# Small query tiles first in the attention, a denser rest of the query projection, and 16 high-part copies moved from ScalarE to VectorE

## The chip, the cores and the metric

The kernel runs on one core of one Trainium2 chip. The metric is the device time of one execution in microseconds (us). A core has engines that run side by side, each working through its own instructions in order: TensorE (PE, matrix products and transposes; PEld is its weight load), VectorE (DVE), ScalarE (ACT), GpSimd (POOL) and SyncE (SP, here only a queue of transfers). TensorE writes to PSUM, and VectorE and ScalarE read its results there.

## What is computed

The reference is a two-layer decoder trunk over 512 positions of width 1024, all in float32. Layer 0 mixes with a gated recurrence and a retention, layer 1 with a sparse attention of three branches; each layer ends in a SwiGLU feed-forward part. The change lies in the attention of layer 1. For each query position it computes three attentions and adds them with gates:

```
s = einsum('bqgrd,bngd->bgrqn', qb, kc)            # compressed keys, 31 of them
o_cmp = softmax(s, masked) @ vc
s = einsum('bqgrd,bgqkld->bgrqkl', qb, kg)         # selected blocks: all 8 blocks are selected (top_k = 8)
o_slc = softmax(s, causal) @ vg
s = einsum('bqgrd,bkgd->bgrqk', qb, kw)            # window of 512 positions
o_win = softmax(s, causal) @ vw
o = gb[..., 0:1] * o_cmp + gb[..., 1:2] * o_slc + gb[..., 2:3] * o_win
out = o @ w_out
```

There are 16 heads in 4 groups that share keys and values. With 512 positions the selected and the window branch both come to plain causal attention, each with its own keys and values. They are called branch 0 and branch 1 below.

## The kernel before

Float32 products are made of three products of a reduced type: each operand is split into a high part (a copy that rounds) and a low part (operand minus high part), and high times high, high times low and low times high are added in PSUM (`mm3`, lines 201 to 203). ScalarE makes most high parts and VectorE most low parts.

The 512 queries are four tiles of 128. A query tile `i` sees `i + 1` key blocks of 128, so tile 0 is small and tile 3 large. `attention` cuts the work into units: one group of 4 heads of one tile, with one branch (tiles 2 and 3) or with both (tiles 0 and 1). That makes 4 units for each of tiles 0 and 1, 8 for each of tiles 2 and 3, 24 in all. The order is `tiles = halves[0] + halves[1]`, before (2, 3, 1, 0).

The main loop counts `n` over units. In each step it goes through slots `sl`, at least four. A slot does, in the order of the code: a score of one head of unit `n` (`head_s`, lines 1160 to 1162: two products against the keys' high and low part and one that adds the causal mask, into a tile `ps_s`); for one block of unit `n - 3` (`LAG = 3`) four transposes of probabilities into `ps_tr` (`block_t`, L1185); the score's maximum on VectorE (`head_m`, `nm`, L1166); the high part of the transposed block on ScalarE (`block_hi`, `pth`, L1189); the exponentials on ScalarE, with their sums (`head_e`, `prob`, L1170); the block's low part on VectorE (`block_lo`, `ptl`, L1192); the scaling of one head of unit `n - 1` on GpSimd (`scale`, L1180); and two products of an earlier block into the output (`block_v`, `ps_o`, L1200 and L1201). After a group's last block `finish` adds the two halves of the output (`up` on ScalarE, `o` on VectorE, L1217, two instructions of 64 rows) and splits it (`oh` on ScalarE, `ol` on GpSimd).

Two side streams run in the slots. `side` holds generators that advance one or two steps a slot: the compressed branch of a tile (`compressed`, `pcmp`, lines 1099 to 1131), `finish`, and `late(t)`, which transposes and splits the queries of a later tile (stacking, `qs`, L1017, L1022, L1023). `fill` is the second half of the query projection (heads 8 to 15), tile by tile, 24 products a tile into `ps_t`; one step is 6 products or the taking over of a finished tile. Before, one step of `fill` is done in a slot. The queries of `halves[0]` are stacked as soon as they are projected, three steps late (`flush`); those of `halves[1]` are kept in `qlate` until `late(t)`.

The code's order is not the last word: a scheduler orders each engine's instructions, with the hints of `prio`. The probabilities' tiles share the pool `wr` (4 buffers) with the raw weights, so the first weights of the output projection (`w1o`, then `ps_p`, lines 201 to 203) are loaded when the first of the last four units has been transposed, and then split (`whi` L136 on ScalarE, `wlo` L137 on VectorE).

Of the kernel before, what the change touches and what calls it, by code (L numbers as in the profile page):

```python
# [63 lines left out]
class Trunk:  # L64
# [773 lines left out]
    def layer1(self, hg):  # L838
        nc, a, tc = self.nc, self.a, self.tc
        V, A, Q, T = nc.vector, nc.scalar, nc.gpsimd, nc.tensor  # L840
# [164 lines left out]
            VV.append(vv)  # L1005


        halves = ((2, 3), (1, 0))
        QS = {t: self.b8([P, H, P], F32R, name="qs") for t in halves[0]}
        qlate = self.b8([P, 2, H, DH], name="qlate")  # L1010

# [14 lines left out]
        def by_tile(w, ts):  # L1026
            for t in ts:
                ps = self.psA("ps_t")
                cc = slice(t * P, (t + 1) * P)
                for k0 in range(0, KD, 2):  # L1030
                    self.mm3(ps, [(HH(k)[:, cc], HL(k)[:, cc]) + w[k // 4].at(k % 4 * S, (k % 4 + 1) * S) for k in (k0, k0 + 1)], k0 == 0, k0 == KD - 2)
                    yield t, None
                flush(0)
                yield t, ps

        def queries(c, tiles):
            for t, ps in tiles:
                if ps is None:
                    if c == 0:
                        flush()  # L1040
                    yield
                    continue
                late = t in halves[1]
                qt = qlate[:, halves[1].index(t), 8 * c:8 * c + 8, :] if late else self.g2([P, 8, DH], name="qt")
                A.activation(qt, ps.rearrange("p (h d) -> p h d", h=8), AF.Copy, scale=r8[:, t:t + 1])
                self.rope(qt, 8, self.pcos[:, t, :], self.psin[:, t, :])
                if not late:
                    deferred.append((now, lambda t=t, qt=qt: stack(t, qt.rearrange("p h d -> p (h d)"), c)))
                yield
            if c:  # L1050
                flush(0)
# [3 lines left out]
        fill = queries(1, by_tile([self.unit(), self.unit()], halves[0] + halves[1]))  # L1055
# [22 lines left out]
    def attention(self, QS, stack, stacked, qlate, halves, KH, KL, VV, kc2, vc, gate, OH, OL, fill):  # L1078
# [3 lines left out]
        V, A, Q, T = nc.vector, nc.scalar, nc.gpsimd, nc.tensor  # L1082
# [52 lines left out]
        def late(t):  # L1135
            QS[t] = self.b8([P, H, P], F32R, name="qs")
            for c in range(2):
                stack(t, qlate[:, halves[1].index(t), 8 * c:8 * c + 8, :].rearrange("p h d -> p (h d)"), c)
                yield
# [11 lines left out]
        def head_s(u, r):  # L1151
            if r == 0:
                u.p = self.probs().rearrange("p (r b x) -> p r b x", r=R, b=u.n)
                u.rs = self.sm.tile([P, R, u.n], F32, tag="rs", name="rs")
                u.kh, u.kl = (x[u.g // 2][:, u.bs[0]:u.bs[-1] + 1, u.g % 2, 0:u.nk] for x in (KH, KL))
            h = R * u.g + r
            ps = self.psA("ps_s")
            u.ps = ps[:, 0:u.n * u.nk].rearrange("p (b x) -> p b x", b=u.n)
            q = QS[u.i][:, h, :]
            T.matmul(u.ps, q, u.kh, start=True, stop=False)  # L1160
            T.matmul(u.ps, q, u.kl, start=False, stop=False)
            T.matmul(u.ps[:, :, u.i * P:u.nk], self.identr, self.triNeg.unsqueeze(1).broadcast_to([P, u.n, P]), start=False, stop=True)

        def head_m(u, r):
            u.nm = self.sm.tile([P, 2], F32, tag="nm", name="nm")
            V.tensor_reduce(u.nm[:, 0:u.n], u.ps, axis=AX.X, op=ALU.max, negate=True)  # L1166

        def head_e(u, r):
            for b in range(u.n):
                A.activation(u.p[:, r, b, 0:u.nk], u.ps[:, b, :], AF.Exp, bias=u.nm[:, b:b + 1], accum_out=u.rs[:, r, b:b + 1])  # L1170
# [11 lines left out]
        def block_t(u, b, j):  # L1182
            u.pt = self.psC("ps_tr")
            for r in range(R):
                T.transpose(u.pt[:, r * P:(r + 1) * P], u.p[:, r, b, j * P:(j + 1) * P], self.ident)  # L1185
            u.th, u.tl = (self.g2([P, S], F32R, name="pt" + n) for n in "hl")

        def block_hi(u, b, j):
            A.copy(u.th, u.pt)  # L1189

        def block_lo(u, b, j):
            V.tensor_tensor(u.tl, u.pt, u.th.bitcast(F32), op=ALU.subtract)  # L1192
            u.last = u.th, u.tl
# [36 lines left out]
        def advance():  # L1230
            if side and next(side[0], 0) == 0:
                side.pop(0)
                advance()

        LAG = 3
        prio = self.tc.high_priority
        pend = []
        for n in range(len(units) + LAG):
            us = units[n] if n < len(units) else None
            un = units[n - 1] if 0 <= n - 1 < len(units) else None  # L1240
            uv = units[n - LAG] if n >= LAG else None
            if us is not None and us.g == us.bs[0] == 0:
                at = tiles.index(us.i)
                if at + 1 < NT:
                    t = tiles[at + 1]
                    side += ([late(t)] if t in halves[1] else []) + [compressed(t)]
            nb = len(uv.blocks) if uv else 0
            for sl in range(max(R, nb)):
                hd = us.heads[sl] if us and sl < R else None
                bl = uv.blocks[sl] if sl < nb else None  # L1250
                while us and (us.i, us.g // 2) not in stacked:
                    if next(fill, 0) == 0:
                        advance()
                if hd:
                    head_s(*hd)
                if bl:
                    block_t(*bl)
                if hd:
                    with prio(offset=12):
                        head_m(*hd)  # L1260
                if bl:
                    block_hi(*bl)
                if hd:
                    with prio(offset=-6):
                        head_e(*hd)
                if bl:
                    with prio(offset=-12):
                        block_lo(*bl)
                if un and sl < R:
                    if sl == 0:  # L1270
                        with prio(offset=-6):
                            norm(un)
                    scale(un, sl)
                if len(pend) >= 2:
                    args = pend.pop(0)
                    block_v(*args)
                    u, b, j = args[:3]
                    if u.bs[b] == 1 and j == u.i:
                        side.insert(0, finish(u.i, u.g))
                if bl:  # L1280
                    pend.append(bl + uv.last)
                for _ in range(2 if len(side) > 2 else 1):
                    advance()
                next(fill, 0)
        while pend:
            block_v(*pend.pop(0))
        while side:
# [136 lines left out]
```

## Time and profile before

| | us |
|---|---|
| median of 3 runs (lowest to highest) | 1250.39 (1248.1 to 1251.37) |
| the profiled execution | 1249.32 |
| its span in the trace | 1247.3 |
| TensorE products busy in the span | 1224.3 (98%) |
| TensorE weight loads busy | 1034.7 (83%) |
| VectorE busy | 800.6 (64%) |
| ScalarE busy | 679.8 (54%) |
| GpSimd busy | 231.6 (19%) |

The span is the trace's; the profiled execution's time lies 2.0 us above it. Times in the trace count from the span's start. Shares over the whole span are means over stages of different kinds, so what the attention does is read from its own stretch, 674 to 853 us. In the trace, the durations of instructions that follow each other on an engine overlap; how far is read from their starts.

### The profile page before, as it was taken

To read this page: it belongs to the slowest core of one execution; us is meant where nothing else is said; L and a number is where in the kernel's file an instruction comes from. 1 tells how busy PE (TensorE), PEld (TensorE's weight loads), DVE (VectorE), ACT (ScalarE), POOL (GpSimd) and SP (SyncE) were. 2 spreads that over 40 slices of the span, in tenths; PEclk is the share of its full clock that TensorE was granted. 3 is DMA by queue.
4 is the path that set the end of the run, shared out by engine and by line. 5 is a ranking of instruction groups with operands and counts; after the bars stand their busy time and mean duration, and the time that the engine had idled before them with its cause. 6 is when DMAs were issued, how large, how long until landed. Compare 5 with 4: busy or idle time off the path is not lost.

```text
span 1247.3 us, 16450 instructions
## 1 busy us (share of the span) xinstructions
PE 1224.3 (98%) x6077; PEld 1034.7 (83%) x6077; DVE 800.6 (64%) x1247; ACT 679.8 (54%) x1385; POOL 231.6 (19%) x303
## 2 busy tenths in 40 slices
PE   9999999999999999999999999999999999999996
PEld 7688888888888889987888878877888888889986
DVE  6886629666356636674364889986776546654765
ACT  6541337664256426655454688995666336633651
POOL 0000420220012002100000568680111011101200
PEclk9999999999999999999999999999999999999998
DMA  8121043784478438852100000133488358825832
GB/s 341 68 101 68 35 169 102 172 185 150 102 182 184 134 69 177 223 198 75 66 35 1 1 1 1 35 122 150 113 191 198 110 125 184 195 89 103 180 84 68
DMA packets 35567, 149.23 MB, mean 120 GB/s; under 512 B 3968, under 2 KB 6288, under 8 KB 26656
## 3 DMA queue, kind: packets, MB, share of 16 engines
q1 hardware_dynamic: 21472, 100.91, 22.8%
q0 software_dynamic: 14016, 47.27, 21.4%
q8 instruction: 48, 0.79, 0.3%
q14 instruction: 31, 0.25, 0.1%
HBM read 143.98 MB, written 4.19 MB: 119 GB/s over the span
## 4 chain that ended last, share of the span: by engine, by line
PE 87%; ACT 5%; DVE 3%; DMA 1%; issue 1%; POOL 1%; POOLq 0%; SPq 0%; DVEq 0%; ACTq 0%
PE ps L201 6%; PE ps L203 6%; PE ps L202 6%; PE ps_t L201 5%; PE ps_t L203 5%; PE ps_t L202 5%; PE ps_X L201 5%; PE ps_X L203 4%; PE ps_X L202 4%; PE ps_V L201 3%; PE ps_V L202 3%; PE ps_V L203 3%; PE ps_Z L202 2%; PE ps_Z L201 2%; PE ps_Z L203 2%; PE ps_Y L201 2%
## 5 line engine op out<-in xcount | busy, mean ns | idle before, releaser
L136 ACT CAST whi<-wr 128x512 fp32r<-128x512 f32 (+1 forms) x540 | 295.2, 593 | 349.8 <-PE ps L202 125.1
L137 DVE TENSOR_TENSOR wlo<-wr,whi 128x1024 fp32r<-128x1024 f32 (+2 forms) x272 | 313.2, 1154 | 207.6 <-ACT whi L136 204.7
L201 PE MATMUL ps<-gh,whi 128*128 128x512 f32 (+1 forms) x364 | 139.9, 384 | 0.0
L203 PE MATMUL ps<-gh,wlo 128*128 128x512 f32 (+1 forms) x364 | 139.3, 383 | 0.0
L202 PE MATMUL ps<-gl,whi 128*128 128x512 f32 (+1 forms) x364 | 139.1, 382 | 0.0
L161 POOL DMA_DIRECT2D wr<-wff x64 | 55.4, 866 | 367.1 <-DVE wlo L137 332.7
L201 PE MATMUL ps_t<-whi,hgh 128*128 128x512 f32 x288 | 114.8, 399 | 0.0
L202 PE MATMUL ps_t<-wlo,hgh 128*128 128x512 f32 x288 | 113.4, 394 | 0.0
L203 PE MATMUL ps_t<-whi,hgl 128*128 128x512 f32 x288 | 112.7, 391 | 0.0
L201 PE MATMUL ps_X<-whi,sg 128*128 128x512 f32 (+1 forms) x288 | 107.3, 373 | 0.6 <-DVE part L290 0.6
L203 PE MATMUL ps_X<-whi,sg 128*128 128x512 f32 (+1 forms) x288 | 107.0, 371 | 0.0
L202 PE MATMUL ps_X<-wlo,sg 128*128 128x512 f32 (+1 forms) x288 | 106.8, 371 | 0.0
L1180 POOL TENSOR_TENSOR prob<-prob,rs 128x384 f32<-128x384 f32 (+3 forms) x128 | 88.0, 721 | 1.9
L765 DVE TENSOR_TENSOR h<-ps,h 128x512 f32<-128x512 f32 x46 | 31.8, 691 | 82.7 <-PE ps L203 82.7
L203 PEld LDWEIGHTS ps<-gh,wlo 128*128 128x128 f32 x364 | 68.4, 188 | 13.4
L202 PEld LDWEIGHTS ps<-gl,whi 128*128 128x128 f32 x364 | 68.5, 188 | 13.1
L201 PEld LDWEIGHTS ps<-gh,whi 128*128 128x128 f32 x364 | 68.5, 188 | 13.0
L1170 ACT ACTIVATE prob<-ps_s,nm 128x384 f32<-128x384 f32 (+3 forms) x128 | 68.1, 540 | 15.8 <-DVE nm L1166 14.7
L201 PE MATMUL ps_V<-whi,sg 128*128 128x512 f32 (+1 forms) x192 | 71.5, 372 | 0.0
L203 PE MATMUL ps_V<-whi,sg 128*128 128x512 f32 (+1 forms) x192 | 71.2, 371 | 0.0
L202 PE MATMUL ps_V<-wlo,sg 128*128 128x512 f32 (+1 forms) x192 | 71.2, 371 | 0.0
L203 PEld LDWEIGHTS ps_t<-whi,hgl 128*128 128x128 f32 x288 | 54.1, 188 | 11.5 <-issue 0.2
(314 smaller groups left out, 2568.9 us busy)
## 6 DMA issues: line engine op xcount, KB each, us to landing
wr<-wff POOLq DMA_DIRECT2D x64, 512.0 KB, 5.7
wr<-wff SPq DMA_DIRECT2D x24, 1024.0 KB, 4.8
wr<-wfg POOLq DMA_DIRECT2D x32, 384.0 KB, 5.9
wr<-w0t SPq DMA_DIRECT2D x10, 1024.0 KB, 6.1
wr<-w1t SPq DMA_DIRECT2D x10, 1024.0 KB, 4.8
wr<-wfg SPq DMA_DIRECT2D x12, 768.0 KB, 4.3
wr<-w2a SPq DMA_DIRECT2D x8, 1024.0 KB, 4.8
wr<-w2c SPq DMA_DIRECT2D x8, 1024.0 KB, 5.0
```

The source lines that it names most:

```text
L136: self.nc.scalar.copy(hi[:, c], x[:, c])
L137: self.nc.vector.tensor_tensor(lo, x, hi.bitcast(F32), op=ALU.subtract)
L161: self.nc.gpsimd.dma_start(x[:, c], more[:, c], accum_op=ALU.add)
L201: mm(ps, ah, bh, start=(first and k == 0), stop=False)
L202: mm(ps, ah, bl, start=False, stop=False)
L203: mm(ps, al, bh, start=False, stop=(last and k == n - 1))
L765: V.tensor_tensor(hm, ps, hm, op=ALU.add)
L1170: A.activation(u.p[:, r, b, 0:u.nk], u.ps[:, b, :], AF.Exp, bias=u.nm[:, b:b + 1], accum_out=u.rs[:, r, b:b + 1])
L1180: Q.tensor_tensor(x, x, u.rs[:, r, b:b + 1].broadcast_to([P, u.nk]), op=ALU.mult)
```

## The change

Three lines change. The tiles go in the order (0, 1, 2, 3), and now tiles 0 and 1 are stacked at once and tiles 2 and 3 late. In steps `n < 3` a slot does two steps of `fill`. And the high part of a transposed block goes to VectorE for all blocks of tile 0 and for every second one of tile 1.

```
-        halves = ((2, 3), (1, 0))
+        halves = ((0, 1), (2, 3))
         def block_hi(u, b, j):
-            A.copy(u.th, u.pt)
+            if u.i == 0 or u.i == 1 and (b + j) % 2:
+                V.tensor_copy(u.th, u.pt)
+            else:
+                A.copy(u.th, u.pt)
-                next(fill, 0)
+                for _ in range(2 if n < LAG else 1):
+                    next(fill, 0)
```

Lines behind `block_hi` move down by four: `ptl` is L1196 in the changed kernel, the output sum L1221, the output products L1204 and L1205; the copy on VectorE is L1191.

On TensorE, where the first blocks of probabilities are transposed (`ps_s` a score, `ps_tr` transposes, `ps_t` the filler), before has in a row:

```order
L1160 MATMUL ps_s<-kh,qs 128x384
L1161 MATMUL ps_s<-kl,qs 128x384
L1162 MATMUL ps_s<-triNeg,identr 128x128
L1185 MATMUL ps_tr<-ident,prob 128x128 x4
L201 MATMUL ps_t<-whi,hgh 128x512
L202 MATMUL ps_t<-wlo,hgh 128x512
L203 MATMUL ps_t<-whi,hgl 128x512
```

And the changed kernel, from the last score of tile 0 (256 columns) to the first of tile 1 (512 columns):

```order
L1160 MATMUL ps_s<-kh,qs 128x256
L1161 MATMUL ps_s<-kl,qs 128x256
L1162 MATMUL ps_s<-triNeg,identr 128x256
L1204 MATMUL ps_o<-pth,vv 128x512
L1160 MATMUL ps_s<-kh,qs 128x512
L1161 MATMUL ps_s<-kl,qs 128x512
L1162 MATMUL ps_s<-triNeg,identr 128x2x128
```

The filler stood between transposes of the first tile; now all 96 of its products stand ahead of the first transposes, and none is left when tile 1 begins.

On VectorE, in the stage of tile 1 (`nm` a maximum, `ptl` a low part, `pcmp` the compressed branch, `o` the output sum, `rs` the reciprocal of a sum), before has in a row:

```order
L1192 TENSOR_TENSOR ptl<-ps_tr,pth 128x512
L1103 TENSOR_TENSOR pcmp<-ps_s,tab 128x4x64
L1166 TENSOR_REDUCE nm<-ps_s 128x2
L1104 TENSOR_TENSOR pcmp<-ps_s,pcmp 128x4x64
L1192 TENSOR_TENSOR ptl<-ps_tr,pth 128x512
L1166 TENSOR_REDUCE nm<-ps_s 128x2
L1192 TENSOR_TENSOR ptl<-ps_tr,pth 128x512
L1217 TENSOR_TENSOR o<-ps_o,up 64x256 x2
```

And the changed kernel in the same stage, which now comes second:

```order
L1174 RECIPROCAL rs<-rs 128x8
L1196 TENSOR_TENSOR ptl<-ps_tr,pth 128x512
L1103 TENSOR_TENSOR pcmp<-ps_s,tab 128x4x64
L1191 CAST pth<-ps_tr 128x512
L1104 TENSOR_TENSOR pcmp<-ps_s,pcmp 128x4x64
L1166 TENSOR_REDUCE nm<-ps_s 128x2 x2
L1196 TENSOR_TENSOR ptl<-ps_tr,pth 128x512
L1166 TENSOR_REDUCE nm<-ps_s 128x2
L1221 TENSOR_TENSOR o<-ps_o,up 64x256 x2
```

The high part (`CAST`) now stands on VectorE among the maxima, ahead of its own low part; 16 such casts stand there in all, 2 before the first maximum of tile 1, 8 in its stage and 6 in that of tile 2.

On VectorE at the end of the attention (`wlo` is a low part of the output projection's weights, `h` the sum behind that projection), before has in a row:

```order
L1192 TENSOR_TENSOR ptl<-ps_tr,pth 128x512 x2
L1217 TENSOR_TENSOR o<-ps_o,up 64x256 x2
L1192 TENSOR_TENSOR ptl<-ps_tr,pth 128x512 x2
L1217 TENSOR_TENSOR o<-ps_o,up 64x256 x4
L137 TENSOR_TENSOR wlo<-wr,whi 128x1024 x4
L1072 TENSOR_TENSOR h<-ps_p,h 128x512
```

And the changed kernel, at the same end, now that of tile 3:

```order
L1196 TENSOR_TENSOR ptl<-ps_tr,pth 128x512 x6
L137 TENSOR_TENSOR wlo<-wr,whi 128x1024
L1196 TENSOR_TENSOR ptl<-ps_tr,pth 128x512
L1221 TENSOR_TENSOR o<-ps_o,up 64x256 x2
L137 TENSOR_TENSOR wlo<-wr,whi 128x1024
L1196 TENSOR_TENSOR ptl<-ps_tr,pth 128x512
L137 TENSOR_TENSOR wlo<-wr,whi 128x1024
L1196 TENSOR_TENSOR ptl<-ps_tr,pth 128x512 x2
L137 TENSOR_TENSOR wlo<-wr,whi 128x1024
L1196 TENSOR_TENSOR ptl<-ps_tr,pth 128x512 x2
L1221 TENSOR_TENSOR o<-ps_o,up 64x256 x2
L1072 TENSOR_TENSOR h<-ps_p,h 128x512
```

The four weight splits stood behind the last output sum; now they stand between the low parts.

## Rows read from the trace of the kernel before

**Rows 1.** Busy time, share of the span and instructions of each engine.

```profile
PE 1224.3 (98%) x6077; PEld 1034.7 (83%) x6077; DVE 800.6 (64%) x1247; ACT 679.8 (54%) x1385; POOL 231.6 (19%) x303
```

**Rows 2.** Stages: us, busy (instructions) of PE, PEld, DVE, ACT, POOL; clock; DMA.

```profile
678.05:730.27 52.22, 50.66 (x313) 45.66 (x312) 43.00 (x91) 36.77 (x94) 27.61 (x39) 1.00 0.00 1
730.27:783.69 53.42, 50.52 (x303) 41.15 (x303) 48.86 (x93) 45.54 (x107) 39.00 (x47) 1.00 0.01 1
783.69:812.65 28.96, 28.61 (x177) 24.02 (x176) 26.75 (x49) 27.46 (x88) 19.72 (x33) 1.00 0.17 53
812.65:834.70 22.05, 21.66 (x142) 18.31 (x141) 19.86 (x45) 21.89 (x84) 19.20 (x44) 1.00 0.12 35
...
848.40:853.00 4.60, 4.60 (x13) 3.68 (x14) 3.87 (x3) 0.00 (x0) 0.52 (x1) 0.63 0.33 135
```

**Rows 3.** Timeline, TensorE ahead of the attention: start, us, instruction (first, 20th after).

```profile
656.17 0.39 PE L202 MATMUL ps_t<-wlo,hgh 128*128 128x512 f32 x1
...
660.70 0.39 PE L201 MATMUL ps_t<-whi,hgh 128*128 128x512 f32 x1
```

**Rows 4.** VectorE groups by form: count | busy us, mean ns | idle before, releaser.

```profile
L1192 DVE TENSOR_TENSOR ptl<-ps_tr,pth 128x512 fp32r<-128x512 f32 x80 | 54.3, 680 | 7.0 <-ACT pth L1189 5.9
L1166 DVE TENSOR_REDUCE nm<-ps_s 128x1 f32<-128x512 f32 x32 | 21.6, 682 | 2.6 <-PE ps_s L1162 2.1
L1166 DVE TENSOR_REDUCE nm<-ps_s 128x1 f32<-128x384 f32 x32 | 17.5, 549 | 4.2 <-PE ps_s L1162 4.0
L1217 DVE TENSOR_TENSOR o<-ps_o,up 64x256 f32<-64x256 f32 x32 | 13.2, 414 | 2.3 <-ACT up L1212 2.1
...
L1166 DVE TENSOR_REDUCE nm<-ps_s 128x2 f32<-128x256 f32 x16 | 6.7, 418 | 0.2
...
L933 DVE COPY t<-ps_tr 64x512 f32<-64x512 f32 x4 | 2.7, 682 | 5.8 <-PE ps_tr L931 5.7
```

**Rows 5.** Timeline, VectorE in the stage of tile 3, a low part and its follower.

```profile
751.14 0.68 DVE L1192 TENSOR_TENSOR ptl<-ps_tr,pth 128x512 fp32r<-128x512 f32 x1
751.74 0.68 DVE L1166 TENSOR_REDUCE nm<-ps_s 128x1 f32<-128x512 f32 x1
```

**Rows 6.** ScalarE: the high-part group, and two exponentials in the timeline of tile 0.

```profile
L1189 ACT CAST pth<-ps_tr 128x512 fp32r<-128x512 f32 x80 | 47.2, 590 | 2.5 <-PE ps_tr L1185 1.6 <-POOL prob L1180 0.2
...
816.42 0.37 ACT L1170 ACTIVATE prob<-ps_s,nm 128x128 f32<-128x128 f32 x1
...
816.78 0.36 ACT L1170 ACTIVATE prob<-ps_s,nm 128x128 f32<-128x128 f32 x1
```

**Rows 7.** Timeline, TensorE at the attention's start; in brackets idle before and releaser.

```profile
674.31 1.04 PE L1017 MATMUL ps_tr<-ident,qt 128*128 128x128 f32 x8
676.50 0.44 PE L1160 MATMUL ps_s<-kh,qs 128*128 128x384 f32 x1 [1.15 <-DVE qs L1023]
...
678.45 0.34 PE L1160 MATMUL ps_s<-kh,qs 128*128 128x384 f32 x1
...
680.30 0.33 PE L1160 MATMUL ps_s<-kh,qs 128*128 128x384 f32 x1
```

**Rows 8.** Timeline, TensorE in the stage of tile 3: a wait for GpSimd.

```profile
736.25 0.66 PE L1128 MATMUL ps_tr<-ident,pcmp 128*128 128x128 f32 x4 [1.74 <-POOL pcmp L1122]
```

**Rows 9.** Timeline at the attention's end: transfers, ScalarE's first weight split, TensorE.

```profile
833.45 5.84 SPq L117 DMA_DIRECT2D wr<-w1o  x3
...
838.61 0.62 ACT L136 CAST whi<-wr 128x512 fp32r<-128x512 f32 x1
...
848.38 0.50 PE L203 MATMUL ps_p<-oh,wlo 128*128 128x512 f32 x1 [2.58 <-DVE wlo L137]
...
849.74 0.63 PE L202 MATMUL ps_p<-ol,whi 128*128 128x512 f32 x1
850.16 0.63 PE L203 MATMUL ps_p<-oh,wlo 128*128 128x512 f32 x1
```

**Rows 10.** A stretch of 10 us inside the stage of tile 3, columns as in rows 2.

```profile
750.00:760.00 10.00, 9.91 (x57) 8.00 (x57) 9.92 (x20) 8.55 (x23) 7.89 (x10) 1.00 0.01 2
```

## The prediction

> **What bounds the kernel now.** I read the engine totals first, then the attention of layer 1 cut into stages, then what each engine does in a stage, and last the waits of TensorE at both ends. The totals put TensorE at 98% of the span [rows 1], and the change leaves every matrix product as it is, so it can only move TensorE's pauses. The attention is the place: I cut it at the first score maximum of each query tile (678.05 tile 2, 730.27 tile 3, 783.69 tile 1, 812.65 tile 0; the last maximum at 834.70) [rows 2]. These four stages are 156.65 us. By its matrix products TensorE is busy in them 50.66 + 50.52 + 28.61 + 21.66 = 151.45 us, by its weight loads 129.1 us. In the tile 3 stage VectorE is busy 48.86 of 53.42 us, ScalarE 45.54; in the tile 0 stage ScalarE is busy 21.89 of 22.05 us. So each stage has its own bound, and three engines lie close together.
>
> How much TensorE could give depends on which of its two rows is believed. By the Trainium skill ("Perfetto Trace Analysis", Identifying the Most-Contended Engine) matmul busy time is a poor measure, since products are pipelined, and weight-load time is a better one: by the products' row 5 us could be won in the four stages, by the weight loads' row 27 us. This case's rows side with the page: 20 products of 512 columns start 4.53 us apart, 0.227 each, though each is shown as 0.39 [rows 3]; I count TensorE by 0.227.
>
> **Prices.** A group's mean overlaps the next instruction by 0.08 on VectorE: a low part shown as 0.68 us is followed 0.60 later [rows 4, 5]. So, start to start: low part 0.60, maximum over 512 columns 0.60, over 384 0.47, over two times 128 0.34; a half of an output sum stays at 0.41 [rows 4]. On ScalarE a high-part copy costs 0.48 (0.59 less 0.11), and an exponential of 128 columns with its accumulator read 0.36 [rows 6].
>
> **The 16 copies.** The condition moves the high parts of all 8 blocks of tile 0 and of 8 of the 16 blocks of tile 1; tiles 2 and 3 keep theirs on ScalarE. The trace of before has no such copy of 128 partitions on VectorE. Its bounds are ScalarE's 0.48 and the undiscounted 0.68; I take 0.60, since the nearest row, a VectorE copy out of PSUM with 512 columns, shows 682 ns [rows 4] like the low part. That is 9.6 us more on VectorE (7.7 to 10.9) and 7.7 us less on ScalarE. Behind each copy wait, on VectorE, the low part of the same block and the maxima of the next scores, and TensorE waits for both.
>
> **The order of the tiles, stage by stage.** I count what the changed program has on each engine between the first maxima, by the prices above.
> - Stage tile 0 (16 slots, now with all the filler). TensorE: 96 filler products 21.8, 48 score products of 256 columns 5.5, the rest 2.5, together 29.8 us; VectorE 21.6, ScalarE 17.0. TensorE sets it. In before a slot of 3 score products and 6 filler products took 1.85 us (678.45 to 680.30) against 1.77 by columns [rows 7], 4% over; with the seven slots that have no filler paced by ScalarE (two times 0.36) I take 32 us.
> - Stage tile 1 (16 slots). VectorE: 16 maxima 9.6, 8 copies 4.8, 11 low parts 6.6, 8 halves of output sums 3.3, compressed branch 4.9, the rest 1.2: 30.4 us. ScalarE 22.7, TensorE 22.0. VectorE sets it.
> - Stage tile 2 (32 slots, its late queries and those of tile 3). VectorE: 32 maxima 15.0, 26 low parts 15.6, the last 6 copies 3.6, 12 halves of output sums 4.9, 7 stackings 4.8, compressed branch 6.5, reciprocals 0.7: 51.1 us. ScalarE 39.1, TensorE 38.4.
> - Stage tile 3 (32 slots, nothing beside). VectorE 39.9, ScalarE 38.8, TensorE 38.7.
>
> The same count for before gives its fullest engine 47.5 (VectorE) in the tile 3 stage, 27.2 (ScalarE) in tile 1 and 22.1 (ScalarE) in tile 0, that is 0.89, 0.94 and 1.00 of the measured stages [rows 2]. The 0.89 holds a pause of 1.74 us in which TensorE waited for GpSimd's compressed probabilities [rows 8]. I take 0.92 for the three stages in which VectorE leads, between the two nearest: 33.0 + 55.5 + 43.4. With 32 this makes 163.9 us, against 156.65.
>
> **The start.** Before, stacked queries of tile 2 came late: 24 filler products and 8 transposes stand ahead of the first score, and then it waits 1.15 us [rows 7]. In the changed order tiles 0 and 1 are the first two that the projection delivers, so 24 products fewer (5.4 us) stand ahead, and only 4 transposes directly in front, with one product group between the two stackings; of the 2.19 us from 674.31 to 676.50 I leave 0.7. The first maximum thus moves 6.9 us forward, to 671.1, and the last falls at 671.1 + 163.9 = 835.0: 0.3 us later than now.
>
> **The tail.** Before, after the last maximum, 6 blocks remain; then VectorE comes to the weight splits of the output projection only behind the last output sums, TensorE waits 2.58 us for them, and then eight products start 0.42 apart [rows 9] instead of 0.227, near half the full 2.4 GHz (the granted clock is 0.63 on average over 848.40 to 853.00 [rows 2]), about 1.6 us lost. At 853.0, 18.3 us after the last maximum, 21 projection products are done. In the changed order 13 blocks remain, but four weight splits stand between the low parts and 19 projection products between the transposes. VectorE has 13 low parts 7.8, 4 splits 4.8, 3 sums 2.5: 15.2 us; ScalarE stands about 1.3 us for the first weights, whose load is issued at the block before (in before 5.2 us from the issue at 833.45 to the first split at 838.61 [rows 9]), and its 8 split copies push the casts back: I take 17.7, and 0.8 for the last products, 18.5. Two products fewer (0.45) and a last wait of 0.7 for the final output make the tail 1.3 us longer; without ScalarE's stand it is 1.1 shorter. I put 1.0 into the sum. TensorE's long wait goes, so the clock should not fall there; that is counted in the 18.5.
>
> **Sum.** 0.3 + 1.0 = +1.3 us. The profiled execution took 1249.32 (span 1247.3 and 2 us around it), the median 1250.39; on the median that is 1251.7, and I say 1251.5. About 0.3% (3.75 us) is what a measurement of this kernel can tell from no change, so this counts as no change.
>
> **Rivals.**
> - *VectorE keeps 97%, faster.* From 750 to 760, inside the tile 3 stage, VectorE is busy 9.92 of 10 us [rows 10]; if its order stays that dense in the three stages they take 31.3 + 52.7 + 41.1, with 31 for the first 156.1, and the last maximum falls at 827.2. With the tail that is about -6.5: 1244. For it: ScalarE and TensorE both have slack in tiles 1 and 2, and no filler interrupts. Against: in no stage of before did VectorE's counted work fill more than 0.9 of the time. A page leads here too: the Trainium skill ("TensorEngine Tiling (Array Packing)", PSUM Bottleneck) says to use ScalarE and VectorE both for emptying PSUM. The trace agrees for the tile 0 stage, where ScalarE is full, and not for the rest, where VectorE is the fuller. It decides above a share of 0.95. Chance 0.32.
> - *The copies lengthen VectorE's stages, slower.* If a block's high and low part, now one behind the other on VectorE, leave it at 0.88, as in the tile 3 stage of before with its pause, the stages take 33 + 34.5 + 58.1 + 45.3 = 170.9, the last maximum falls at 842: +7.3 with a tail as long as now, 1258. For it: 9.6 us are added to the engine that already has most in those stages, and GpSimd's in-order scalings gave just such a pause. Against: the filler has left them, so nothing else competes on TensorE. It decides below 0.90. Chance 0.28.
> - That the change does less than it says can be left out: 16 casts stand on VectorE in the changed order, and all filler ahead of the first tile 1 score.
>
> **How the numbers follow.** The forecast, a share between 0.90 and 0.95, has 0.40; faster 0.32; slower 0.28. The range takes the rivals' prices with a microsecond beyond, 1243 to 1259; only the far ends of both rivals, less than 2 in 10, lie outside.
>
> **What would show it.** Right: first maximum near 671; 16 casts on VectorE of some 0.68; VectorE busy over 9 of 10 in the tile 1 and 2 stages, with ScalarE clearly below; about 55 us for tile 2 and 43 for tile 3; no wait over 2 us for the projection's weights and no fallen clock there. Wrong: a tile 1 or 2 stage in which TensorE waits mostly for ScalarE or GpSimd, a tile 3 stage well off 43 us, or a first load of the output projection that comes later than the casts need it.

## The result, and the profile after

The changed kernel takes 1261.38 us (median of 4 runs) against 1249.6: a ratio of 1.0091, 95% interval 1.0076 to 1.0106, 11 us slower. The prediction said 1251.5, in a range of 1243 to 1259. Its profiled execution took 1261.12 us with a span of 1259.2, 11.9 more than before.

The page's first block, the totals by engine (compare [rows 1]): 16 instructions have moved from ScalarE to VectorE, which is 5.8 us busier, ScalarE 5.4 less, and TensorE's share has not changed.

```profile
PE 1230.1 (98%) x6077; PEld 1037.3 (82%) x6077; DVE 806.4 (64%) x1263; ACT 674.4 (54%) x1369; POOL 231.2 (18%) x303
```

The stages of the changed kernel, cut like [rows 2] at the first score maximum of each tile (tile 0, 1, 2, 3; the last row ends at the last maximum). Columns: us, then busy us of PE, PEld, DVE, ACT, POOL, then TensorE's granted clock and the DMA's share and GB/s.

```profile
672.39:706.91 34.52, 34.06 (x189) 29.14 (x188) 22.33 (x58) 21.74 (x79) 9.89 (x27) 1.00 0.00 1
706.91:739.63 32.72, 27.34 (x143) 21.01 (x142) 29.84 (x62) 23.98 (x80) 27.11 (x52) 0.95 0.00 1
739.63:798.08 58.45, 50.21 (x310) 43.03 (x311) 52.39 (x108) 40.87 (x104) 32.89 (x47) 0.98 0.08 24
798.08:844.22 46.14, 45.81 (x277) 38.93 (x275) 40.77 (x74) 41.34 (x100) 35.41 (x44) 0.99 0.05 18
```

They sum to 171.83 us where before had 156.65 and the prediction 163.9. The first maximum is 5.66 us earlier, the four stages are 15.18 longer, and from the last maximum to the end of the span it is 414.98 against 412.6, 2.38 longer: 15.18 + 2.38 - 5.66 = 11.9, the whole difference. Of the start, 1.68 us belong to the run and not to the change: the last transposes of stacked keys, which both kernels reach by the same instructions, stand at 650.72 before and 652.40 after. Among all profiled runs of this study that point lies between 649.79 and 652.94 without a pattern, so a difference of up to 3 us between the spans of two single profiles says nothing; the medians decide.

By its row of products, TensorE stood idle for 5.2 us of the four stages before and for 14.4 us after. Its waits between the first and the last maximum follow (line that waits, releaser, total us, times, longest). Before had four kinds, with 4.6 us in all, of which 3.0 for GpSimd:

```profile
PE ps_tr L1128 <- POOL pcmp L1122: 1.7, 1, 1.7
PE ps_tr L1185 <- DVE ptl L1192: 1.4, 5, 0.5
PE ps_tr L1128 <- POOL prob L1180: 1.3, 1, 1.3
```

In the changed kernel it is 14.0 us in all; most of it carries VectorE's name, and one single wait is 2.2 us long:

```profile
PE ps_tr L1185 <- DVE ptl L1196: 6.5, 9, 2.2
PE ps_s L1160 <- ACT prob L1170: 1.9, 4, 0.7
PE ps_o L1204 <- DVE pth L1191: 1.3, 3, 0.6
```

That 2.2 us wait carries VectorE's name, but VectorE was not busy. The next four fences are the timeline of the changed kernel shortly before tile 3's first score (start, us, instruction; in brackets the idle time before it and what ended it). GpSimd scales probabilities, and the subtraction of the compressed branch's maximum stands behind that, though the maximum that it subtracts was made on VectorE by 787.59:

```profile
786.91 0.68 DVE L1107 TENSOR_REDUCE mx<-pcmp 128x16 f32<-128x512 f32 x1
...
787.79 2.41 POOL L1180 TENSOR_TENSOR prob<-prob,rs 128x384 f32<-128x384 f32 x3
...
790.15 1.05 POOL L1109 TENSOR_TENSOR pcmp<-pcmp,mx 128x512 f32<-128x512 f32 x1
```

ScalarE takes its instructions in order; the compressed exponential stands ahead of the next unit's, and so ScalarE stands for 2.27 us:

```profile
791.24 0.63 ACT L1111 ACTIVATE pcmp<-pcmp 128x512 f32<-128x512 f32 x1 [2.27 <-POOL pcmp L1109]
791.78 0.56 ACT L1170 ACTIVATE prob<-ps_s,nm 128x384 f32<-128x384 f32 x1
```

VectorE's next instruction is the reciprocal of a sum which that exponential delivers, with the low parts behind it:

```profile
792.46 0.18 DVE L1174 RECIPROCAL rs<-rs 128x4 f32<-128x4 f32 x1 [2.16 <-ACT prob L1170]
...
793.60 1.28 DVE L1196 TENSOR_TENSOR ptl<-ps_tr,pth 128x512 fp32r<-128x512 f32 x2
```

And TensorE waits for a low part to free a buffer; a little later its products start 0.43 apart, as long as at 1.2 GHz, in place of 0.23:

```profile
794.42 0.63 PE L1185 MATMUL ps_tr<-ident,prob 128*128 128x128 f32 x4 [2.22 <-DVE ptl L1196]
...
796.41 0.63 PE L1205 MATMUL ps_o<-ptl,vv 128*128 128x512 f32 x1
796.84 0.63 PE L1160 MATMUL ps_s<-kh,qs 128*128 128x512 f32 x1
```

Two stretches of the changed kernel with the clock below 1.00, columns as in the stages: one at the end of the tile 1 stage, behind four waits of 0.53 to 0.89 us within 4.5 us, and the one just shown. Each takes about 0.43 of 4 us from TensorE, 1.7 us; where another engine leads, the kernel need not lose as much.

```profile
734.00:738.00 4.00, 3.51 (x15) 3.07 (x16) 2.23 (x5) 1.97 (x6) 3.92 (x8) 0.57 0.02 4
795.00:799.00 4.00, 4.00 (x16) 3.52 (x15) 3.78 (x9) 2.08 (x7) 2.30 (x4) 0.57 0.48 152
```

Before had no such stretch in its four stages and one in its tail [rows 2]; that one is gone.

### The profile page after: what moved, and what is told of

It reads as the page before. It is cut to its first block, busy times and chain, and to the rows that moved or that the text cites. A ratio compares the mean times of both kernels' runs of the same rounds, so it can differ in the third digit from the quotient of the medians.

```text
span 1259.2 us, 16458 instructions
## 1 busy us (share of the span) xinstructions
PE 1230.1 (98%) x6077; PEld 1037.3 (82%) x6077; DVE 806.4 (64%) x1263; ACT 674.4 (54%) x1369; POOL 231.2 (18%) x303
## 4 chain that ended last, share of the span: by engine, by line
PE 88%; DVE 6%; ACT 2%; POOL 1%; issue 1%; DMA 1%; SPq 0%; POOLq 0%; DVEq 0%; ACTq 0%
PE ps L201 6%; PE ps L203 6%; PE ps L202 6%; PE ps_t L201 5%; PE ps_t L203 5%; PE ps_t L202 5%; PE ps_X L201 5%; PE ps_X L203 5%; PE ps_X L202 5%; PE ps_V L201 3%; PE ps_V L203 3%; PE ps_V L202 3%; PE ps_Y L201 2%; PE ps_Z L201 2%; PE ps_Y L203 2%; PE ps_Z L203 2%
## 5 line engine op out<-in xcount | busy, mean ns | idle before, releaser
L1180 POOL TENSOR_TENSOR prob<-prob,rs 128x128 f32<-128x128 f32 (+3 forms) x128 | 88.0, 722 | 1.7
L1170 ACT ACTIVATE prob<-ps_s,nm 128x128 f32<-128x128 f32 (+3 forms) x128 | 67.2, 530 | 25.8 <-DVE nm L1166 23.3
L201 PEld LDWEIGHTS ps_t<-whi,hgh 128*128 128x128 f32 x288 | 54.1, 188 | 11.7 <-ACT tok_v L515 0.6
```

What stands on the lines that cost most here:

```text
L201: mm(ps, ah, bh, start=(first and k == 0), stop=False)
L1180: Q.tensor_tensor(x, x, u.rs[:, r, b:b + 1].broadcast_to([P, u.nk]), op=ALU.mult)
```

## Experiments: which of the three edits costs

The change has three edits: the order of the tiles, the dense filler, the copies. Medians below stand beside runs of the kernel before on the same chip, at 1248.9 to 1249.7 us.

**The change without the copies** (order and dense filler):

```diff
-            if u.i == 0 or u.i == 1 and (b + j) % 2:
-                V.tensor_copy(u.th, u.pt)
-            else:
-                A.copy(u.th, u.pt)
+            A.copy(u.th, u.pt)
```

> The changed kernel with all high-part copies back on ScalarE; new tile order and dense filler stay. Theory A (the 16 copies lengthen the stages that VectorE leads): 16 times 0.60 = 9.6 us leave VectorE, which was busy 29.8 of 32.7 us in the tile 1 stage and 52.4 of 58.5 in the tile 2 stage; the time falls by 7 to 10 us, to 1251 to 1254, and the tile 1 and tile 2 stages are shorter by about that. Theory B (the order is to blame: the filler is spent in the tile 0 stage, and the stages behind it pause at the changes of tile, whoever copies): within 3 us of the changed kernel, 1258 to 1262.

Measured 1254.89 us, ratio 1.0044 (1.0032 to 1.0056). The copies cost 1.0091 less 1.0044, 5.9 us, a little less than theory A asked for; the other 5.5 us stay, so B holds too. Its stages:

```profile
670.46:704.02 33.56, 32.98 (x183) 28.00 (x182) 21.36 (x57) 21.76 (x78) 8.92 (x25) 1.00 0.00 1
704.02:735.15 31.13, 27.35 (x150) 20.88 (x148) 26.12 (x54) 27.95 (x94) 26.48 (x52) 1.00 0.01 2
735.15:790.15 55.00, 49.56 (x310) 42.86 (x311) 48.69 (x102) 43.02 (x110) 34.35 (x50) 0.98 0.08 24
790.15:836.29 46.14, 45.78 (x277) 38.95 (x275) 40.71 (x74) 41.30 (x100) 35.36 (x44) 0.99 0.05 19
```

In the tile 2 stage VectorE has 3.70 us less than in the changed kernel and the stage is 3.45 shorter; in the tile 3 stage nothing differs.

**The copies alone**, in the old order (the same condition put into the kernel before):

> The kernel before with the 16 copies on VectorE and nothing else; here they fall into its last two stages. Theory A: VectorE, 26.8 of 29.0 us busy in the tile 1 stage and 19.9 of 22.1 in the tile 0 stage, gets 4.8 us more in each and leads them; about 6 us slower, 1254 to 1258. Theory B: ScalarE was the full engine in the tile 0 stage (21.9 of 22.1) and is relieved by the same copies; within 2 us of before, 1248 to 1252.

Measured 1249.28 us, ratio 1.000 (0.999 to 1.0009). Theory A falls as a rule for any place: here the same 16 copies are free. Ten of them lie in the stages of tiles 1 and 0, which grew by 1.3 us together (29.49 and 22.80 against 28.96 and 22.05), and the tail gave it back: TensorE's 2.58 us wait for split weights [rows 9] is not there any more, nor the fallen clock behind it.

**The order alone** (`halves = ((0, 1), (2, 3))` and nothing else):

> The kernel before with only the order of the query tiles changed to 0, 1, 2, 3; copies on ScalarE, one filler step in a slot. Theory A: no loss, since nothing is added to VectorE: 1246 to 1252. Theory B: most of the loss is there already: 1256 to 1261; the waits of TensorE stand at the two changes to a late tile (tile 1 to 2, tile 2 to 3).

Measured 1254.67 us, ratio 1.0056 (1.0043 to 1.0069), between the two theories and nearer to B. The dense filler next to the order changes nothing that can be told (1.0044). So the loss is: order 5.5 to 7 us, copies 6 us, and copies cost only in the new order.

## Experiments: the filler

**No filler beside the attention.** In both orders, with copies on ScalarE and one filler step in a slot, the whole projection is run first:

```diff
+        for _ in fill:
+            pass
         self.attention(QS, stack, stacked, qlate, halves, KH, KL, VV, kc2, vc, gate, OH, OL, fill)
```

> The new order, one filler step in a slot and ScalarE's copies, but the whole query projection is done before the first score: nothing lies beside the attention. It pays 96 products at 0.227, 21.8 us, ahead and gets back what the filler cost in the tile 0 stage. Theory B1 (the order loses because the filler lies in a stage where VectorE and ScalarE have little to do): the tile 0 stage falls from 34 to about 24 us, and the difference to the kernel before with its filler ahead is under 3 us: 1263 to 1267 against 1260 to 1264. Theory B2 (the order loses in the attention itself, in the later stages and the drain): the difference stays at 5 us or more.

> The kernel before with the whole query projection ahead of the first score: 72 products at 0.227, 16.4 us, go ahead of it, and the tile 2 stage keeps VectorE's 43.0 us, at a share of 0.9 that is 47.8 in place of 52.2: 12 us slower, 1260 to 1264. Theory B1: within 3 us of the new order with its filler ahead. Theory B2: at least 5 us below it.

New order 1257.07 us, ratio 1.0058 (1.0036 to 1.008); old order 1254.33, ratio 1.004 (1.0026 to 1.0054). Both losses were much smaller than expected, and the difference is 2 to 3 us, theory B1's side, though by the two intervals B2's 5 us are not excluded. Stages of the new order with their sum, then tile 2's stage of the old order and the sum of all its stages:

```profile
692.90:712.30 19.40, 15.60 (x87) 13.51 (x87) 12.53 (x36) 15.26 (x69) 11.29 (x29) 0.82 0.00 1
712.30:742.05 29.75, 25.24 (x136) 19.95 (x134) 24.73 (x48) 24.80 (x83) 21.65 (x41) 0.94 0.00 1
742.05:793.78 51.73, 50.66 (x326) 43.77 (x325) 49.37 (x106) 45.30 (x118) 36.48 (x54) 1.00 0.08 26
793.78:839.63 45.85, 44.21 (x271) 37.74 (x269) 40.60 (x75) 40.96 (x100) 35.58 (x45) 1.00 0.06 19
sum 146.73, PE 135.71 PEld 114.97 DVE 127.23 ACT 126.32 POOL 105.00; mean PE 33.93 PEld 28.74 DVE 31.81 ACT 31.58 POOL 26.25
```

```profile
693.08:735.49 42.41, 37.94 (x233) 33.36 (x233) 34.68 (x79) 32.59 (x88) 28.34 (x40) 0.96 0.00 1
...
sum 147.54, PE 138.55 PEld 117.19 DVE 129.57 ACT 127.59 POOL 105.20; mean PE 46.18 PEld 39.06 DVE 43.19 ACT 42.53 POOL 35.07
```

Without filler the attention is as long in either order, 146.7 and 147.5 us. With it, the old order's stages are 156.65 us for 72 products of 16.4 us: by the sums, 7.3 us of the filler are hidden. The new order's are 165.83 (dense) or 167.80 (one step) for 96 products of 21.8 us: by the sums, only 0.7 to 2.7 us are hidden. It is tempting to conclude that filler is hidden beside tile 2 and not beside tile 0, as theory B1 has it, but the stages say otherwise. The dense filler lengthens tile 0's stage by 14.2 us (33.56 against 19.40), and in the old order the filler lengthens tile 2's stage by 9.8 (52.22 against 42.41). So 7.6 and 6.6 us are hidden, about as much in either place. Without the filler, TensorE loses 3.5 and 1.7 us there to a fallen clock (0.18 of 19.4 us, 0.04 of 42.4), which the filler spares it.

What the new order loses on top stands in stages that hold no filler in either run: tile 1's takes 31.13 us behind the dense filler and 29.75 with the filler ahead, tile 2's 55.00 and 51.73. In tile 2's stage TensorE waits 5.1 us in the first, with a wait of 2.2 us as in the changed kernel, and 0.8 us in the second. VectorE has four stackings there in the second and seven in the first, since part of the late queries is stacked earlier. So B1's number came, but not by B1's reason; why the pause goes with the filler ahead was not followed. The Trainium skill ("Perfetto Trace Analysis", Optimization Strategy) advises to interleave stretches that have different most-contended engines; the two stages agree, with 7.6 of 21.8 us and 6.6 of 16.4 hidden.

**Filler at half the rate**, in every second slot, to bring it beside fuller slots (`if sl % 2: next(fill, 0)`). First in the changed kernel, then without the copies, then in the old order with tile 0's copies on VectorE:

> The changed kernel with a filler step in every second slot, in place of two in each of the first 12 slots: about 48 of the 96 filler products move behind the first 16 slots, into the tile 1 stage. Theory A: the tile 1 stage is VectorE's own and stays at 33 us with the filler hidden in it, the tile 0 stage falls from 34.5 us to 25 to 28: 1252 to 1255. Theory B (the filler is cover for pauses that are chains of waits): the same gain and a tile 1 stage without a pause over 0.5 us: 1250 to 1254. A rival to both: filler in the tile 1 stage delays VectorE's inputs, and the gain is given back: 1259 to 1263.

> The new order, all copies on ScalarE, and a filler step in every second slot; to be compared with the same kernel with the dense filler (1254.9 us) and with the half-rate one with copies (1259.2). Theory B1 (VectorE-led tile 1 stage hides filler once the copies are gone): 1250 to 1253. Theory D (the half-rate filler lost because TensorE's pauses, of which it had three with a fallen clock, come from the order): 1255 to 1258.

> The order of before, tile 0's eight copies on VectorE, and a filler step in every second slot: the 72 products beside tile 2 lie over 28 slots in place of 16. Theory B1 (filler is worth most where VectorE leads and TensorE has pauses): with all of it ahead, the run before showed that 16.4 us of products were 5.4 us dearer, so 11 us of them were not hidden; the second half of the tile 2 stage, where VectorE is busy 8.7 to 9.3 of 10 us, hides more of them: 2 to 4 us under the same kernel with one step in a slot, 1243 to 1246. Rival: TensorE pauses in the first slots, which have no blocks yet, and its clock falls: 1248 to 1252.

Measured 1259.21 (1.0086), 1258.09 (1.0069, 1.0055 to 1.0083) and 1252.83 (1.0024, 1.0015 to 1.0033). None gains; the second is 3 us dearer than with dense filler, the third 5 us dearer than its partner below (1247.69). So B1 as a recipe, to lay the filler where VectorE leads, fell. A likely reason is that slow filler delivers the queries late. In the second TensorE waits for stacked queries at the start, which the dense one does not:

```profile
PE ps_s L1160 <- DVE qs L1023: 3.3, 3, 1.6
```

But its four stages sum to 166.14 us, only 0.3 above the dense filler's, and of the 3.2 us between the two profiles' spans 2.5 lie ahead of the attention; so the profiles do not show where the median's 3 us are lost. In the third the stages are 160.54 us against its partner's 156.39, so there the loss lies in the attention. Theory D did not explain the second either, since that profile shows the clock at 1.00 throughout the attention.

## Experiments: GpSimd's queue

The chain in the timeline above can be cut without touching order or copies: the compressed branch's subtraction goes to VectorE, so that ScalarE's exponential no longer stands for GpSimd's scalings.

```diff
-            Q.tensor_tensor(pc, pc, mx.unsqueeze(2).broadcast_to([P, H, 32]), op=ALU.subtract)
+            V.tensor_tensor(pc, pc, mx.unsqueeze(2).broadcast_to([P, H, 32]), op=ALU.subtract)
```

**New order, dense filler, no copies, with this:**

> The new order with dense filler, all copies on ScalarE, and the same subtraction on VectorE. Theory Q: the pause of 2.2 us before tile 3's first scores and the fallen clock behind it (1.8 us) go, VectorE pays 2 us: 1251 to 1254. Theory S (VectorE's amount of work in the tile 2 stage sets it, and the pause only moves): 1255 to 1257.

Measured 1250.26 us, ratio 1.0008 (0.9999 to 1.0017): 4.5 us of the order's 5.5 are back, 3.5 of them in the four stages (162.33 us against 165.83). VectorE and ScalarE at the same place (timeline); the wait of 2.27 us is gone:

```profile
780.16 0.79 DVE L1109 TENSOR_TENSOR pcmp<-pcmp,mx 128x512 f32<-128x512 f32 x1
```

```profile
780.99 0.63 ACT L1111 ACTIVATE pcmp<-pcmp 128x512 f32<-128x512 f32 x1
```

Its tile 1 and 2 stages: 1.4 and 2.0 us shorter than without the move, at a clock of 1.00, though VectorE has 0.5 us more in each; tile 1's is now as long as with the filler ahead (29.75). VectorE is busy 0.93 of the tile 2 stage, where it was 0.89 with the pause:

```profile
704.06:733.83 29.77, 26.93 (x150) 20.91 (x149) 26.63 (x56) 28.25 (x94) 25.45 (x49) 1.00 0.01 1
733.83:786.84 53.01, 49.40 (x317) 42.88 (x318) 49.25 (x103) 43.57 (x111) 31.76 (x47) 1.00 0.08 24
```

**The same with the copies, that is the changed kernel with the subtraction moved:**

> The changed kernel, copies and all, with the compressed branch's subtraction of its maximum on VectorE in place of GpSimd. Theory Q2 (the queue of GpSimd and the copies are two losses that add: without copies the move gave 4.6 us): 1255.5 to 1258. Theory A+ (the copies cost 6 us through VectorE's amount of work in the tile 1 and 2 stages, and VectorE's 2 us more now cost in full, the pause being elsewhere): 1259 to 1263. Theory Q3 (the copies cost only by way of the same pauses and fallen clocks): 1250 to 1253.

Measured 1259.31 us, ratio 1.008 (1.0068 to 1.0092): theory A+. Against the run before, the copies now cost 9.0 us, nearly the full 16 times 0.60. Its tile 1 and 2 stages:

```profile
704.15:737.75 33.60, 27.78 (x145) 21.28 (x143) 30.50 (x63) 24.15 (x80) 27.37 (x52) 0.95 0.00 1
737.75:794.82 57.07, 50.18 (x317) 42.93 (x318) 53.38 (x110) 41.41 (x105) 29.91 (x43) 1.00 0.08 23
```

VectorE is 3.87 and 4.13 us busier, and the stages are 3.83 and 4.06 us longer (the first with a fallen clock again). So the copies lengthen VectorE's stages one for one. The changed kernel itself gains nothing clear of noise by the move (1.008 against 1.0091), so the queue and the copies are not two losses that add: with the copies in place VectorE is busy 0.94 of the tile 2 stage once the pause is gone, and little is left to win. That the copies cost only 5.9 us beside the pause, part of their cost being masked by it, fits this, but the intervals of 5.9 and 9.0 overlap.

**Both of GpSimd's compressed products on VectorE** (the scaling at L1122 too), **and the single move with one filler step in a slot:**

> The new order with dense filler, all copies on ScalarE, and both of the compressed branch's products of 128x512 that GpSimd had (the subtraction of the maximum and the scaling) on VectorE. Theory Q: the two waits that are left for GpSimd's compressed probabilities (1.2 us in the profile of the run with one of them moved) go, and VectorE pays 2 us more, in stages that it leads: 1249 to 1252. If GpSimd's order were the whole of what is left of the order's loss: 1247 to 1248.

> The new order with one filler step in a slot, all copies on ScalarE, and the subtraction on VectorE; beside the same with the dense filler (1250.3 us). Theory Q says that the order's loss of 5.8 us at this rate of the filler (1254.7) has the same cause: 1249 to 1252. If the dense filler is a part of the recovery: 1253 to 1255.

Measured 1251.25 (1.0018, 1.0007 to 1.0029) and 1253.99 (1.0044, 1.0028 to 1.006). The second product gains nothing (stages of 162.62 us against 162.33). And at one step in a slot the move brings back only 1.5 of the 7 us, which the intervals do not tell from nothing: there TensorE still waits once for 1.9 us for GpSimd's scaling and 1.4 for queries. What the move is worth thus depends on the filler's rate, as the second expectation had it; why the order loses the rest at that rate was not followed further.

**In the old order** (tile 0's copies on VectorE, and the move):

> The order of before, tile 0's eight copies on VectorE, and the compressed branch's subtraction of its maximum (four of 1.05 us on GpSimd, behind its scalings) on VectorE, four of about 0.6. Theory Q (ScalarE's compressed exponential stands for GpSimd's queue, and with it every exponential behind it): TensorE's 1.74 us wait at the first compressed transposes goes, VectorE pays about 2 us in stages that it half leads: 1245 to 1248, at or under the same kernel without the move. Rival: VectorE is the dearer place, 1249 to 1251.

Measured 1247.88 us, ratio 0.9989 (0.998 to 0.9998), no different from its partner without the move, which comes next (0.9983). The old order has the same queue; TensorE's wait for compressed probabilities there fell only from 1.74 to 1.2 us, and VectorE is 1.5 us busier in the tile 3 stage. So the time lay in theory Q's range, but not by its mechanism.

## Experiments: where a copy is free

**Only tile 0's eight copies, in the old order** (`if u.i == 0:` as the condition):

> The kernel before with only the eight copies of tile 0 on VectorE; six of them belong to the blocks behind the last maximum. Theory A (a copy costs where VectorE leads, and is free or a gain where ScalarE is late): in the drain ScalarE's weight splits and copies stand one behind the other, VectorE had room, and TensorE's 2.58 us wait for the split weights goes with the fallen clock behind it (1.6 us), as in the run with all 16 copies, whose stages of tiles 1 and 0 were 1.3 us longer: 1245 to 1248. Theory C (the gain at the drain in that run was chance): 1248 to 1251.

Measured 1247.69 us, ratio 0.9983 (0.997 to 0.9995): with its partner above the only version that is under both kernels, here by 0.05 to 0.3%. At the end TensorE's longest wait is 0.8 us, for an output's high part, where before had 2.58:

```profile
PE ps_p L201 <- ACT oh L1224: 0.8, 1, 0.8
PE ps_tr L1185 <- DVE ptl L1195: 0.8, 2, 0.5
```

**Eight copies of tile 3, in the new order** (`if u.i == 3 and j == 3:`, dense filler):

> The new order with dense filler, and eight copies on VectorE, but those of tile 3 (the last block of each of its units) in place of those of tiles 0 and 1; to be compared with the same kernel without copies (1254.9 us). Theory T (TensorE sets the tile 3 stage: a slot of it takes 1.43 us by its products and transposes, 32 of them 45.8 of 46.1 us): five of the eight copies fall into that stage, VectorE goes from 40.7 to 44 us, and the time stays within 1 us: 1253.5 to 1256. Theory V (VectorE sets it at a share of 0.88, as the prediction had it): the stage grows by 5 times 0.60 over 0.88, 3.4 us, and with the drain the time is 1258 to 1260.

Measured 1256.74 us, ratio 1.0053 (1.0035 to 1.0071), 1 us over the kernel without copies: between the theories, near T. The tile 3 stage took 45.89 us in place of 46.14, with VectorE at 42.26 and not 40.71:

```profile
791.77:837.66 45.89, 44.42 (x263) 36.62 (x261) 42.26 (x78) 38.52 (x93) 33.60 (x42) 1.00 0.05 17
```

VectorE does not set that stage: in the runs of this order the stage takes 44.8 to 46.2 us, whether VectorE is busy 40.6 or 42.3 of them. One slot of it on TensorE, in the changed kernel:

```profile
841.51 0.40 PE L1160 MATMUL ps_s<-kh,qs 128*128 128x512 f32 x1
841.75 0.39 PE L1161 MATMUL ps_s<-kl,qs 128*128 128x512 f32 x1
841.98 0.22 PE L1162 MATMUL ps_s<-triNeg,identr 128*128 128x128 f32 x1
842.04 0.61 PE L1185 MATMUL ps_tr<-ident,prob 128*128 128x128 f32 x4
842.40 0.48 PE L1204 MATMUL ps_o<-pth,vv 128*128 128x512 f32 x1
842.72 0.39 PE L1205 MATMUL ps_o<-ptl,vv 128*128 128x512 f32 x1
842.95 0.39 PE L1160 MATMUL ps_s<-kh,qs 128*128 128x512 f32 x1
```

From one first score product to the next it is 1.44 us without a pause. Between the first and the last maximum lie 31 slots, 44.6 us if all were like this one; three of them hold no block, and the compressed branch adds eight products and four transposes. That comes near the stage's 46.14 us, and TensorE waits only 0.2 us in it.

## Why the prediction was wrong

The profile lies 10.6 us above the forecast (+11.9 and not +1.3): 7.9 of them in the four stages (tile 0 2.5, tile 1 -0.3, tile 2 3.0, tile 3 2.7), 1.4 in the tail and 1.2 in the start.

**The start was right.** Predicted 6.9 us earlier; 5.66 in the profile, 7.3 without the 1.68 us that this run lost ahead of the attention.

**Tile 0's stage, 32 us, took 34.5.** TensorE sets most of it, as said, and its time was nearly right: from tile 0's first score product (671.41) to tile 1's it is 32.7 us. What failed is the end of the stage. The first maximum of tile 1 comes about 2 us behind its score, because VectorE was busy without a break from 700.4 on, with maxima, two of the copies and the compressed branch:

```profile
704.10 0.39 PE L1160 MATMUL ps_s<-kh,qs 128*128 128x512 f32 x1
```

```profile
704.63 0.68 DVE L1191 CAST pth<-ps_tr 128x512 fp32r<-128x512 f32 x1
...
706.91 0.62 DVE L1166 TENSOR_REDUCE nm<-ps_s 128x2 f32<-128x512 f32 x1
```

The prediction compared VectorE's 21.6 us with the whole stage and did not ask how much of them falls at its end. Without the copies the stage took 33.56.

**Tile 1's stage, 33.0, took 32.7,** with VectorE at 29.84 of the counted 30.4. The term is right, though TensorE lost 1.6 us at its end to a fallen clock (0.05 of 32.72) that the prediction did not have.

**Tile 2's stage, 55.5, took 58.45.** The step that failed is the share of 0.92. VectorE's count held: its row says 52.39 us where 51.1 were counted, but the same row said 48.86 in before where 47.5 were counted, so the two are different measures (one low part was missed, 27 and not 26). By the count the share was 0.87, because the pause behind GpSimd's queue came here with a fallen clock. Without the pause the share would have been right: with the copies and the queue cut, the stage took 57.07 us, and 51.1 with 0.8 for each of the two subtractions that VectorE then has there is 0.92 of it (an estimate). The prediction had seen such a pause before [rows 8] and took it as a reason why 0.89 was too low a share for later. It should have counted how often that chain runs, once for each tile.

**Tile 3's stage, 43.4, took 46.1.** The step that failed is the count of TensorE, 38.7 us. It priced products by 0.227 throughout, but the first product behind four transposes is followed 0.32 later and the transposes take 0.36 together: 1.44 us a slot, where its price gives about 1.19. So TensorE leads this stage, and not VectorE. The prediction sided with the Trainium skill ("Perfetto Trace Analysis", Identifying the Most-Contended Engine), which prefers weight loads to matmul busy time as a measure of TensorE. In this stage the trace disagrees: the weight loads' 38.93 us would promise 7 us of slack, the busy 45.81 of 46.14 say none, and the slot shows that there is none.

**The tail, +1.0, was +2.4.** The wait and the fallen clock went, as predicted. From the last maximum to the 21st product of the output projection it is 20.04 us against 18.03 before. The prediction counted VectorE (15.2, measured 15.60) and ScalarE, and not TensorE, which is the fullest there; that TensorE sets the tail was not tested:

```profile
844.22:864.26 20.04, 18.83 (x103) 14.28 (x102) 15.60 (x24) 13.42 (x28) 6.39 (x8) 1.00 0.67 230
```

**The copies** were priced well where VectorE leads: 9.0 us measured once the pause was out of the way, 5.9 with it. The condition was missing: in the old order they are free, since there ScalarE is the late engine at the end. In the tail of before VectorE waits for it ahead of its last output sum, which holds up the weight splits behind:

```profile
846.07 0.85 DVE L1217 TENSOR_TENSOR o<-ps_o,up 64x256 f32<-64x256 f32 x2 [0.98 <-ACT up L1212]
```

The Trainium skill ("TensorEngine Tiling (Array Packing)", PSUM Bottleneck) says to use both engines for emptying PSUM; tile 0's eight copies agree (0.9983), the sixteen in stages that VectorE led do not.

**The rivals.** What happened is the slower rival, whose stages (170.9 us, with 58.1 and 45.3 for the last two) are nearly those measured in sum, and whose reason, copies that lengthen VectorE's stages while GpSimd's order makes pauses, held in the runs for tile 2. For tile 3 its reason was wrong and its number right by accident, and for tiles 0 and 1 its 33 and 34.5 stand against 34.5 and 32.7, two misses that cancel. It gave 1258 because it left the tail as it was; with the tail's 2.4 it would have been 1260.4. VectorE at 97% did not come near: it was busy 0.91, 0.90 and 0.88 of the three stages. By the prediction's own counts the shares came out at 0.93, 0.87 and 0.87 (30.4, 51.1 and 39.9 over 32.7, 58.5 and 46.1). The one stage of before that VectorE led without filler beside it had 0.89 by the same counts; going up from it to 0.92, halfway to a stage that ScalarE led, had no row behind it.

## What to carry to other kernels

Two sums over several stages do not say where a loss lies: here the sums pointed at the filler's place, and the stages showed that it hid about 7 us beside the small tile as beside the large one, and that the loss behind the dense filler stood in stages without any. A wait's named releaser may itself stand idle: follow the chain back through each in-order queue to an engine that was busy, and cut it there, which here gave back 4.5 of 5.5 us with the copies on ScalarE and the dense filler, and nothing clear of noise with the copies on VectorE, with one filler step in a slot, or in the old order. And the same copies were free where ScalarE was late and cost nearly their whole length where VectorE led, so look at the stage before moving them.

## What the runs showed of the hardware

- A single pause of TensorE of 2.2 us, with products on both sides, was followed by a stretch of about 3.5 us at the lower clock, 1.2 GHz (0.57 of full speed on average over 4 us); four shorter ones close together were followed by such a stretch too. Each took about 1.7 us from TensorE on top of the pause. Several of the kernels above have one, the changed kernel two, and the two fastest none in the attention and its tail.
- The subtraction over 128 by 512 elements takes 1.05 us on GpSimd (mean of four) and 0.78 on VectorE (mean of four in the run without copies); what made GpSimd dear was the 2.4 us of scalings ahead of it in its queue.
- Programs with the same instructions up to a point reached it up to 3.2 us apart in single profiles (649.79 to 652.94).
